# Small matrix products scheduled in unbroken blocks by tile shape, mixer sums of mixed shapes reordered, and 16- and 32-row products padded to 128 rows, in a four-layer forward pass

## The chip, the cores and the metric

The kernel runs on one core of a Trainium2 chip. A core has five engines that run at the same time and wait for each other by semaphores: TensorE (PE, matrix products, with a weight loader PEld beside it), VectorE (DVE), ScalarE (ACT), GpSimd (POOL) and SyncE (SP, which issues most DMAs). The metric is device microseconds of one execution, lower is better. Before the change the median of 3 runs is 991.59 us (989.36 to 992.03).

## The reference, cut to what matters

The input is one sequence of 256 tokens with 1024 features, all in float32. Four layers follow each other:

- Layer 1 (`even_mixer`): two recurrent mixers side by side, gated linear attention (4 heads) and RWKV-7 (8 heads with a 64x64 state each), then a SwiGLU feed-forward.
- Layer 2 (`odd_mixer`): latent attention with 16 heads, causal by chunks of 64, then a feed-forward.
- Layers 3 and 4 (`even_layer`, `odd_layer`): gated attention layers with 6 + 6 heads, or 12 heads, of 64 features, and 4 heads that attend to a memory of 256 rows.

What matters here are the small products. The RWKV-7 recurrence per head and token is

```
sa = jnp.einsum('bhvk,bhk->bhv', state, at)
state = state * wt[:, :, None, :] + sa[..., None] * bt[:, :, None, :] + vt[..., None] * kt[:, :, None, :]
y = jnp.einsum('bhvk,bhk->bhv', state, rt)
```

and attention in layers 3 and 4 is, per head, with positions turned into a bias,

```
s = softmax(q @ k.T * SCALE + bias)      # 256 queries, up to 256 keys, 64 features
o = s @ v
```

Everything else is dense projections against weights that are read from HBM.

## The kernel before, in words

The kernel is not written in the order in which it runs. Calls such as `mm1`, `V.tensor_mul` or `SC.activation` only note an operation in a `Plan` (`note`, line 222). At the end `Plan.schedule` (line 273) places all operations engine by engine in a list schedule: it keeps a clock for each engine, gives each operation a planned cost (`cost`), and picks for each free engine the ready operation with the lowest number whose tiles fit in the free buffers. Instructions are then emitted in that order, and an engine executes them in order on the chip.

Dense projections are done in `fp32r` with the weights and the activations each split in a high and a low part: `mm3` issues three products of 128x128 by up to 512 columns. Small products are single calls (`mm1`) in float32 or `fp32r`, and many of them use only a part of the 128x128 array: 64 or 32 rows of the contraction, 64 or 32 output columns. Which part is used is the tile's shape. `part_of` (line 513) gives it to the planner as rows and columns in steps of 32, 64 and 128. When the shape of an operation differs from the last one, the planner adds `TURN` nanoseconds to its cost, and while the last shape is not the full one it prefers operations of the same shape (`same_part`). Nothing forces products that were written together to run together: wide products of another stream can be placed between them.

Two streams of 128 tokens each, `stream(0)` and `stream(1)`, run interleaved, so that wide products of one fill the waits of the other. PSUM has 8 banks; `ORDER` and `CAP` say how many each group of operations may hold.

The places that the change touches:

- Low-rank gates of layer 1 (from line 1021): `w2a2` holds two 64-row weights in its halves; `g2u` holds a 32-row weight in its rows 0 to 31 and a 16-row one in rows 32 to 47. Their products use 64, 32 and 16 rows of the array.
- RWKV-7, in four chunks `c` of 64 tokens (group `R0` to `R3`): `rw_gram` (line 1202) makes the gram products of a chunk, head half 0 first and then head half 1; `rw_level` and `rw_last` invert a triangular matrix with 32x32 products; `rw_step` (line 1273) carries the state, with sums in PSUM of a 128-row product (`q["m"]` with `v_`) and a 64-row product (`blk(...)` with the old state `z`).
- Gated linear attention, `gla` (line 1362): `blocks` makes 32x32 diagonal blocks from 64-row products, five times, and further levels use similar products.
- `attend` (line 1671): for a round of heads, `points` makes the scores through `scores`, `weights` does the softmax, `turn` transposes, `values` multiplies by the values. `biased` (line 2126) and `attend_c` in `odd` give the `scores` of layers 3 and 4. Head `h` reads the row half `h % 2` of the queries and keys. For the second token tile a score has three passes (high and low parts, `dots`, line 1630).

In `points` the banks of two row halves are filled pair by pair, and inside `scores` the DVE bias follows right behind each pair:

```
for js in zip(*jobs):
    scores(js)
```

All operations on one PSUM tile follow each other in the order in which they are noted, so the second pair's products wait for the first pair's bias.

Of the kernel before, what the change touches and what calls it, by code (L numbers as in the profile page):

```python
# [19 lines left out]
P = 128  # L20
# [32 lines left out]
CAP = {("ps", "mmm"): 8, ("ps", "R0"): 1, ("ps", "R1"): 3, ("ps", "R2"): 3, ("ps", "R3"): 2, ("ps", "Bmm"): 3, ("ps", "B"): 3, ("ps", "Cmm"): 2, ("ps", "Mmm"): 2, ("ps", "M"): 1}  # L53
# [7 lines left out]
TURN = 92.0  # L61
# [119 lines left out]
class Op:  # L181
    __slots__ = ("i", "eng", "meth", "args", "kw", "cost", "dma", "succ", "need", "ready", "new", "vts", "prio",
                 "start", "end", "lab", "follow", "heavy", "busy", "table", "part", "alts", "lock")
# [22 lines left out]
class Plan:  # L206
    def __init__(self):
        self.ops, self.tiles = [], []
        self.group = "m"
        self.prio = 0.0  # L210
        self.cap = {}
        self.order = {}
# [9 lines left out]
    def note(self, eng, meth, args, kw):  # L222
# [8 lines left out]
        op.part = part_of(meth, args) if eng == "tensor" else None  # L231
        op.lock = locks(eng, meth, args, kw)
# [39 lines left out]

    def schedule(self):

        ENG = ("tensor", "vector", "scalar", "gpsimd", "sync")
# [104 lines left out]
        out, pipe, now = [], 0.0, 0.0  # L380
        warm, window, act, level, last = False, 0, {}, 0.0, 0.0
# [4 lines left out]
        while len(out) < n:  # L386
# [3 lines left out]
            for e in ENG:  # L390
                while free_at[e] <= now and (avail[e] or e in STEAL):
                    pick = None
                    if e == "tensor":
# [15 lines left out]
                    op, moved = pick, True  # L409
                    for vt in op.new:  # L410
# [440 lines left out]
def kernel(ctx: ExitStack, tc: tile.TileContext, x, xturn, pos, cols, lowr, wall, mem, memturn, ln_g, ln_b,  # L851
# [172 lines left out]
    glr = T([48, S])  # L1024
    SC.activation(glr[32:48], pss[2][32:48, 0:S], AF.Copy)
# [3 lines left out]
    sg1, sg2 = T([P, S]), T([32, S])  # L1029
# [11 lines left out]
    for j in range(2):  # L1041
        ps = g.ax()
        for d_ in range(2):
            mm1(ps[:, d_ * S:(d_ + 1) * S], w2a2[0:64, (2 * j + d_) * P:(2 * j + d_ + 1) * P], tw)
# [18 lines left out]
        ps = g.ax()  # L1063
        for d_ in range(2):
            mm1(ps[:, d_ * S:(d_ + 1) * S], w2a2[64:128, (2 * j + d_) * P:(2 * j + d_ + 1) * P], al)
# [93 lines left out]
    for j in range(2):  # L1159
# [42 lines left out]
    def rw_gram(c):  # L1202
        m_ = []
        for h in range(2):
            pa = g.ax()
            p4 = pa.rearrange("p (a b c) -> p a b c", a=4, b=2)
            for hp in range(4):
                mm1(p4[:, hp], kb(hp, c, h), blk(ar, slice(0, 2), hp, c, HS[h]))
            m_.append(T([P, 4, 2, 64]))
            V.tensor_mul(m_[h], p4, m64.unsqueeze(1).broadcast_to([P, 4, 2, 64]))  # L1210
# [24 lines left out]
    def rw_level(q, s):  # L1235
        tt = q["tt"]
        w_ = g.ax()[:, 0:P].rearrange("p (a b) -> p a b", b=32)
        for hp, h, j in quarters():
# [5 lines left out]
        for hp, h, j in quarters():  # L1244
            r_ = QS[h][j]
            mm1(d_[r_, hp], wm[r_, hp], tt[r_, 1, hp])
# [5 lines left out]
    def rw_last(q):  # L1252
# [7 lines left out]
        for hp in range(4):  # L1260
# [5 lines left out]
        for hp in range(4):  # L1266
# [6 lines left out]
    def rw_step(q, c, z, yn):  # L1273
# [3 lines left out]
        for hp in range(4):  # L1277
# [9 lines left out]
        for hp, h in PAIRS:  # L1287
# [4 lines left out]
        if c < 3:  # L1292
            pz = g.ax()
            z_ = sl4(pz)
            for hp, h in PAIRS:
# [10 lines left out]
        for hp in range(4):  # L1306
# [55 lines left out]
    def gla():  # L1362
# [11 lines left out]
        for d_ in range(2):  # L1374
            mm1(ps[:, d_ * S:(d_ + 1) * S], gw2[:, d_ * P:(d_ + 1) * P], glr[32:48])
# [18 lines left out]
        def blocks(qq, kk_, fn):  # L1394
            pss = [quarter(g.ax()), quarter(g.ax())]
            for up in range(2):
                for t in range(2):
                    for hp in range(2):
                        for d_ in range(4):
# [7 lines left out]
        for s in range(7):  # L1407
# [11 lines left out]
            if s == 5:  # L1419
# [3 lines left out]
                for t in range(2):  # L1423
# [887 lines left out]
```

## Time and profile before

| what | us |
|---|---|
| median of 3 runs | 991.59 |
| the profiled execution's own time | 986.12 |
| its span, first to last instruction | 984.3 |
| PE busy | 965.1 |
| PEld (weight loads) busy | 817.8 |
| DVE busy | 699.8 |
| ACT busy | 515.3 |
| POOL busy | 129.7 |

Busy time is the union of an engine's instructions. Matmuls overlap in the array and their ends are modelled, so a PE that is shown as busy may still be waiting inside a change of shape. How much work a stretch holds is therefore read from how many products of which shape it contains. A float32 product that is not a transpose stands in the trace as two records, an `fp32r` product or a transpose as one. [...] The mixers of layer 1 run to about 190 us, layer 2's attention lies between about 400 and 515 us, and layers 3 and 4 run from about 712 us to the end.

### The profile page before, as it was taken

To read this page: it belongs to the slowest core of one execution; us is meant where nothing else is said; L and a number is where in the kernel's file an instruction comes from. 1 tells how busy PE (TensorE), PEld (TensorE's weight loads), DVE (VectorE), ACT (ScalarE), POOL (GpSimd) and SP (SyncE) were. 2 spreads that over 40 slices of the span, in tenths; PEclk is the share of its full clock that TensorE was granted. 3 is DMA by queue.
4 is the path that set the end of the run, shared out by engine and by line. 5 is a ranking of instruction groups with operands and counts; after the bars stand their busy time and mean duration, and the time that the engine had idled before them with its cause. 6 is when DMAs were issued, how large, how long until landed. Compare 5 with 4: busy or idle time off the path is not lost.

```text
span 984.3 us, 18847 instructions
## 1 busy us (share of the span) xinstructions
PE 965.1 (98%) x7640; PEld 817.8 (83%) x7640; DVE 699.8 (71%) x1340; ACT 515.3 (52%) x995; POOL 129.7 (13%) x213
## 2 busy tenths in 40 slices
PE   8999999999999999999999999999999999999998
PEld 8977776778999988898877899988777777877777
DVE  8997988797665553876768765554689676777762
ACT  4647543545544443476653555444376664856550
POOL 1113354110000000222310000000022000122000
PEclk9999999999999999999999999999999999999999
DMA  7523434337456453544334664565542324443201
GB/s 250 215 91 136 160 134 162 135 134 256 173 196 225 177 215 112 178 140 154 129 129 169 226 247 172 174 246 181 211 160 97 129 89 170 171 171 130 83 4 44
DMA packets 27495, 156.94 MB, mean 159 GB/s; under 512 B 3424, under 2 KB 4064, under 8 KB 11664
## 3 DMA queue, kind: packets, MB, share of 16 engines
q1 hardware_dynamic: 25408, 150.49, 42.7%
q0 software_dynamic: 1280, 4.20, 1.4%
q8 instruction: 60, 0.98, 0.4%
q10 hardware_dynamic: 720, 1.05, 0.3%
q14 instruction: 27, 0.22, 0.1%
HBM read 154.68 MB, written 1.05 MB: 158 GB/s over the span
## 4 chain that ended last, share of the span: by engine, by line
PE 81%; DVE 9%; ACT 4%; DMA 4%; issue 2%; POOL 0%; SPq 0%; DVEq 0%; ACTq 0%
PE v L828 81%; DVE v L828 9%; DMA v<-in_wall 4%; ACT v L828 3%; ACT L828 1%; POOL v L828 0%; SPq L828 0%; DVEq L828 0%; ACTq L828 0%
## 5 line engine op out<-in xcount | busy, mean ns | idle before, releaser
L828 PE MATMUL v<-v,v 128*128 128x256 f32 (+14 forms) x7620 | 961.1, 295 | 14.9 <-DVE v L828 10.9
L828 PEld LDWEIGHTS v<-v,v 128*128 128x128 f32 (+7 forms) x7620 | 813.7, 164 | 162.1 <-issue 33.0
L828 DVE TENSOR_TENSOR v<-v,v 128x1024 fp32r<-128x1024 f32 (+12 forms) x609 | 462.7, 787 | 179.5 <-ACT v L828 148.1
L828 ACT ACTIVATE v<-v 128x1024 fp32r<-128x1024 f32 (+12 forms) x579 | 396.6, 717 | 355.7 <-PE v L828 180.7
L828 ACT ACTIVATE v<-v,v 128x256 f32<-128x256 f32 (+7 forms) x281 | 119.1, 455 | 96.3 <-PE v L828 67.1
L828 POOL TENSOR_TENSOR v<-v,v 128x4 f32<-128x4 f32 (+8 forms) x95 | 89.2, 951 | 557.5 <-DVE v L828 534.4
L828 DVE SCALAR_TENSOR_TENSOR v<-v,v 128x256 f32<-128x256 f32 (+7 forms) x166 | 67.6, 416 | 46.4 <-ACT v L828 27.9
L828 DVE SCALAR_TENSOR_TENSOR v<-v,v,v 128x128 fp32r<-128x128 f32 (+9 forms) x173 | 78.5, 483 | 9.7 <-PE v L828 5.4
L828 DVE TENSOR_REDUCE v<-v 128x2 f32<-128x512 f32 (+7 forms) x68 | 37.6, 566 | 15.2 <-PE v L828 9.4
L828 DVE COPY v<-v 128x512 f32<-128x512 f32 (+9 forms) x61 | 25.9, 436 | 16.6 <-PE v L828 16.0
L828 POOL DMA_DIRECT2D v<-in_ln_g x8 | 4.8, 598 | 193.1 <-PE v L828 193.1
L828 POOL TENSOR_SCALAR v<-v,v 128x128 f32<-128x128 f32 (+1 forms) x32 | 16.4, 529 | 54.1 <-DVE v L828 54.1
L828 ACT ACTIVATION_READ_ACCUMULATOR v<-v,v 128x1 f32 x96 | 20.1, 209 | 0.0
L828 DVE BATCH_NORM_STATS2 v<-v 128x6 f32<-128x64 f32 (+1 forms) x32 | 14.2, 447 | 2.8 <-PE v L828 2.7
L828 DVE TENSOR_SCALAR v<-v 128x4 f32<-128x4 f32 (+14 forms) x79 | 12.6, 177 | 2.7 <-ACT v L828 2.2
L828 DVE TENSOR_SCALAR v<-v,v 128x4 f32<-128x4 f32 (+6 forms) x42 | 10.4, 257 | 5.0 <-POOL v L828 4.4
L828 ACT ACT_TABLE_LOAD x9 | 11.5, 1283 | 0.9 <-PEq L2300 0.7
L828 POOL COPY v<-v 128x4 f32<-128x4 f32 (+2 forms) x32 | 9.8, 342 | 0.4
L828 DVE CAST v<-v 128x1024 fp32r<-128x1024 f32 (+2 forms) x14 | 8.5, 607 | 0.0
L828 DVE TENSOR_TENSOR v<-v 128x512 f32<-128x512 f32 (+4 forms) x18 | 7.6, 425 | 0.9 <-ACT v L828 0.9
L828 DVE STREAM_TRANSPOSE v<-v 128x128 f32<-128x128 f32 x20 | 5.7, 295 | 0.2
L828 PE MATMUL v<-v 128*128 128x128 f32 x20 | 4.3, 406 | 1.0 <-DVE v L828 1.0
(17 smaller groups left out, 36.1 us busy)
## 6 DMA issues: line engine op xcount, KB each, us to landing
v<-in_wall SPq DMA_DIRECT2D x123, 1024.0 KB, 4.8
v<-in_wall SPq DMA_DIRECT2D x8, 768.0 KB, 4.7
v<-in_wall SPq DMA_DIRECT2D x8, 512.0 KB, 4.3
v<-in_memturn SPq DMA_DIRECT2D x8, 256.0 KB, 5.8
v<-in_ln_g POOLq DMA_DIRECT2D x8, 256.0 KB, 4.1
v<-in_ln_b POOLq DMA_DIRECT2D x8, 256.0 KB, 5.8
v<-in_wall SPq DMA_DIRECT2D x4, 384.0 KB, 2.9
v<-in_mem SPq DMA_DIRECT2D x4, 256.0 KB, 5.5
```

Source lines behind the costliest of these rows:

```text
L828: r = getattr(getattr(nc, op.eng), op.meth)(*[real(x) for x in op.args], **{k: real(x) for k, x in op.kw.items()})
```

## The change

A context `plan.together()` marks matrix products that are noted in it as a block. Before scheduling, `join` makes the first product of a block wait for everything that any product of the block waits for, and gives it all the new tiles of the block. When the planner has placed the first product on PE, the others follow at once (`rest`), with nothing between. The price of a change of shape in the planner goes from 92 to 190, and group `R0` may hold two banks instead of one.

Blocks are put around: the low-rank products of the decay and the gate (now alternating between the two row halves), the gram products (alternating too), each half of an inversion level, each of the four groups of products in `rw_step`, the block products of `gla` (the row half is now the innermost loop), all score products of a round, and the value products of a round. The DVE bias is taken out of `scores` and noted behind the block. The output sum in `rw_step` no longer alternates between 128-row and 64-row products but does all of the one and then all of the other. The 32-row and the 16-row product become 128-row products against a tile `zlr` that is zero in the other rows, and the whole of `g2u` is loaded.

```
-CAP = {..., ("ps", "R0"): 1, ...}
+CAP = {..., ("ps", "R0"): 2, ...}
-TURN = 92.0
+TURN = 190.0
...
+        op.block = None
+        if eng == "tensor" and self.block is not None:
+            op.block = self.block
+            self.block.append(op)
...
+    @contextmanager
+    def together(self):
+        self.block = []
+        yield
+        self.block = None
+
+    def join(self):
+
+        before = {}
+        for o in self.ops:
+            for late, xs in ((True, o.succ), (False, o.follow)):
+                for x in xs:
+                    if x.block is not None and o.block is not x.block and x is not x.block[0]:
+                        before[x.block[0].i, o.i] = before.get((x.block[0].i, o.i), False) or late
+        for (i, j), late in before.items():
+            lead, o = self.ops[i], self.ops[j]
+            if lead not in (o.succ if late else o.succ + o.follow):
+                (o.succ if late else o.follow).append(lead)
+                lead.need += 1
+        for o in self.ops:
+            if o.block is not None and o is not o.block[0]:
+                o.block[0].new += o.new
+                o.new = []
+                if o not in o.block[0].succ:
+                    o.wait_for(o.block[0])
...
-                    if e == "tensor":
+                    if e == "tensor" and rest:
+                        pick = rest.pop(0)
...
+                    if op.block is not None and op is op.block[0]:
+                        rest = op.block[1:]
...
-        SP.dma_start(t_[0:(P, P, 48)[i]], lowr[i, 0:(P, P, 48)[i]])
-    gw2 = g2u[32:48, 0:256]
+        SP.dma_start(t_, lowr[i])
+    zlr = T([P, 2, S])
+    GP.memset(zlr.rearrange("p a b -> p (a b)"), 0.0)
...
-            mm1(o, g2u[0:32, (2 * j + d_) * P:(2 * j + d_ + 1) * P], sg2, False, True)
+            mm1(o, g2u[:, (2 * j + d_) * P:(2 * j + d_ + 1) * P], zlr[:, 0], False, True)
...
-        for h in range(2):
-            pa = g.ax()
-            p4 = pa.rearrange("p (a b c) -> p a b c", a=4, b=2)
-            for hp in range(4):
-                mm1(p4[:, hp], kb(hp, c, h), blk(ar, slice(0, 2), hp, c, HS[h]))
...
+        pa = [g.ax().rearrange("p (a b c) -> p a b c", a=4, b=2) for _ in range(2)]
+        with plan.together():
+            for hp in range(4):
+                for h in range(2):
+                    mm1(pa[h][:, hp], kb(hp, c, h), blk(ar, slice(0, 2), hp, c, HS[h]))
...
-        for hp in range(4):
-            for h in range(2):
-                mm1(y_[HS[h], hp], q["m"][h][:, hp, 1], v_[:, h, hp], True, c == 0)
+
+        with plan.together():
+            for hp, h in PAIRS:
+                mm1(y_[HS[h], hp], q["m"][h][:, hp, 1], v_[:, h, hp], hp == 0, c == 0 and hp == 3)
             if c:
-                for h in range(2):
-                    mm1(y_[HS[h], hp], blk(ar, 1, hp, c, HS[h]), z[HS[h], hp], False, True)
+                for hp, h in PAIRS:
+                    mm1(y_[HS[h], hp], blk(ar, 1, hp, c, HS[h]), z[HS[h], hp], False, hp == 3)
...
-            mm1(ps[:, d_ * S:(d_ + 1) * S], gw2[:, d_ * P:(d_ + 1) * P], glr[32:48])
+            mm1(ps[:, d_ * S:(d_ + 1) * S], g2u[:, d_ * P:(d_ + 1) * P], zlr[:, 1])
...
-            for js in zip(*jobs):
-                scores(js)
+            with plan.together():
+                after = [scores(js) for js in zip(*jobs)]
+            for fn in after:
+                if fn:
+                    fn()
...
-            for h0 in range(first, last, 2):
+            with plan.together():
+              for h0 in range(first, last, 2):
...
-            for h, o in jobs:
-                V.scalar_tensor_tensor(o, dist[:, P - t * P:256], slopes[h], o, op0=OP.mult, op1=OP.add)
+
+            def bias():
+                for h, o in jobs:
+                    V.scalar_tensor_tensor(o, dist[:, P - t * P:256], slopes[h], o, op0=OP.mult, op1=OP.add)
+            return bias
```

What the planner makes of it is seen in PE's order. A row is one product or several equal ones: the tile it writes, the tiles it reads, and the size of its output. The first place is the first round of scores of the second token tile in layer 3. Before, `v_8845` and `v_8847` are the banks of the two row halves, and rows of 128x512 are wide products of projections:

```order
L828 MATMUL v_8845<-v_8683,v_8769 128x256
L828 MATMUL v_8847<-v_8683,v_8769 128x256
L828 MATMUL v_8845<-v_8674,v_8790 128x256
L828 MATMUL v_8847<-v_8674,v_8790 128x256
L828 MATMUL v_8814<-v_8626,v_8421 128x512
L828 MATMUL v_8814<-v_8642,v_8421 128x512
L828 MATMUL v_8814<-v_8626,v_8430 128x512
L828 MATMUL v_8814<-v_8626,v_8421 128x512
L828 MATMUL v_8845<-v_8674,v_8769 128x256
L828 MATMUL v_8845<-v_8683,v_8769 128x256
L828 MATMUL v_8845<-v_8674,v_8790 128x256
L828 MATMUL v_8814<-v_8642,v_8421 128x512
```

Now, with `v_8856` and `v_8857` as the two banks:

```order
L868 MATMUL v_8857<-v_8674,v_8770 128x256
L868 MATMUL v_8856<-v_8683,v_8770 128x256
L868 MATMUL v_8857<-v_8683,v_8770 128x256
L868 MATMUL v_8856<-v_8674,v_8791 128x256
L868 MATMUL v_8857<-v_8674,v_8791 128x256
L868 MATMUL v_8856<-v_8674,v_8770 128x256
L868 MATMUL v_8857<-v_8674,v_8770 128x256
L868 MATMUL v_8856<-v_8683,v_8770 128x256
L868 MATMUL v_8857<-v_8683,v_8770 128x256
L868 MATMUL v_8856<-v_8674,v_8791 128x256
L868 MATMUL v_8857<-v_8674,v_8791 128x256
L868 MATMUL v_8814<-v_8626,v_8430 128x512
```

The twelve score products stood in four pieces with nine wide products between them, and two of the pieces read one row half three times in a row. They now stand in one piece and alternate.

The second place is the output sum of chunk 2 in `rw_step`. Before, `v_2693` is the sum; rows that read `v_1132`, the values, are 128-row products, one for each of two masked gram tiles, and the `x2` rows, which read the old state `v_2587`, are 64-row products:

```order
L828 MATMUL v_2693<-v_1132,v_1260 64x64
L828 MATMUL v_2693<-v_2587,v_831 64x64 x2
L828 MATMUL v_2693<-v_1132,v_1221 64x64
L828 MATMUL v_2693<-v_1132,v_1260 64x64
L828 MATMUL v_2693<-v_2587,v_831 64x64 x2
L828 MATMUL v_2693<-v_1132,v_1221 64x64
L828 MATMUL v_2693<-v_1132,v_1260 64x64
L828 MATMUL v_2693<-v_2587,v_831 64x64 x2
L828 MATMUL v_2748<-v_2443,v_2591 128x512
```

Now, with `v_2966` as the sum:

```order
L868 MATMUL v_2966<-v_1122,v_1991 64x64
L868 MATMUL v_2966<-v_1122,v_2060 64x64
L868 MATMUL v_2966<-v_1122,v_1991 64x64
L868 MATMUL v_2966<-v_1122,v_2060 64x64
L868 MATMUL v_2966<-v_1122,v_1991 64x64
L868 MATMUL v_2966<-v_1122,v_2060 64x64
L868 MATMUL v_2966<-v_1122,v_1991 64x64
L868 MATMUL v_2966<-v_1122,v_2060 64x64
L868 MATMUL v_2966<-v_2371,v_832 64x64 x8
```

The sum alternated between the two shapes in twos; it now has eight products of the one and then eight of the other.

The third place is the gram products of a chunk (`v_1949` and `v_1957` before, `v_1956` and `v_1957` now, one for each row half). Before:

```order
L828 MATMUL v_1676<-v_1653,v_217 128x512
L828 MATMUL v_1941<-v_90,v_841 128x64 x4
L828 MATMUL v_1949<-v_831,v_841 128x128 x4
L828 MATMUL v_1957<-v_831,v_841 128x128 x4
L828 MATMUL v_1966<-v_1885,v_1933 32x32 x16
```

Now:

```order
L868 MATMUL v_1956<-v_832,v_845 128x128
L868 MATMUL v_1957<-v_832,v_845 128x128
L868 MATMUL v_1956<-v_832,v_845 128x128
L868 MATMUL v_1957<-v_832,v_845 128x128
L868 MATMUL v_1956<-v_832,v_845 128x128
L868 MATMUL v_1957<-v_832,v_845 128x128
L868 MATMUL v_1956<-v_832,v_845 128x128
L868 MATMUL v_1957<-v_832,v_845 128x128
L868 MATMUL v_1976<-v_90,v_845 128x64 x4
```

Four products of one row half followed by four of the other have become eight that alternate.

## Rows read from the trace of the kernel before

**Rows 1.** The page: busy us, share of the span, instructions of each engine.

```profile
PE 965.1 (98%) x7640; PEld 817.8 (83%) x7640; DVE 699.8 (71%) x1340; ACT 515.3 (52%) x995; POOL 129.7 (13%) x213
```

**Rows 2.** Stretches: length, busy of PE, PEld, DVE, ACT, POOL, clock, DMA.

```profile
50.00:200.00 150.00, 143.91 (x2504) 112.87 (x2503) 129.44 (x322) 79.15 (x158) 48.87 (x68) 1.00 0.38 135
700.00:950.00 250.00, 247.65 (x1391) 190.90 (x1390) 190.57 (x396) 156.11 (x355) 34.83 (x35) 1.00 0.37 131
```

**Rows 3.** The chain of waits, 700 us to the end: start, us, what.

```profile
712.82 135.19 PE v L828 x735
...
872.60 108.48 PE v L828 x653
```

**Rows 4.** The chain of waits, 102 to 192 us, by line.

```profile
by line: PE v L828 91.1%; DVE v L828 5.6%; ACT v L828 2.8%; issue 1.7%
```

**Rows 5.** Whom PE waits for: us in total, times, longest.

```profile
PE v L828 <- DVE v L828: 12.0, 16, 1.3
PE v L828 <- ACT v L828: 1.8, 2, 1.4
```

**Rows 6.** Groups by shape, 690 to 700 and 600 to 620 us: busy, mean ns.

```profile
L828 PE MATMUL v<-v,v 128*128 128x512 f32 x45 | 10.6, 395 | 0.0
...
L828 PE MATMUL v<-v,v 128*128 128x256 f32 x171 | 20.4, 281 | 0.0
```

**Rows 7.** Weight loader in order of time, 745.5 to 753 us: start, us, idle before.

```profile
747.55 1.08 PEld L828 LDWEIGHTS v<-v,v 64*128 64x128 f32 x6 [0.37 <-issue]
748.99 1.20 PEld L828 LDWEIGHTS v<-v,v 64*128 64x128 f32 x8 [0.36 <-issue]
750.56 0.74 PEld L828 LDWEIGHTS v<-v,v 64*128 64x128 f32 x4 [0.37 <-DVE v L828]
751.54 1.64 PEld L828 LDWEIGHTS v<-v,v 64*128 64x128 f32 x10 [0.24 <-issue]
```

**Rows 8.** Weight loader in order of time, 166 to 173 us.

```profile
166.84 1.14 PEld L828 LDWEIGHTS v<-v,v 32*32 32x32 f32 x36 [0.36 <-DVE v L828]
168.40 1.40 PEld L828 LDWEIGHTS v<-v,v 32*32 32x32 f32 x38 [0.42 <-issue]
170.15 1.14 PEld L828 LDWEIGHTS v<-v,v 32*32 32x32 f32 x36 [0.36 <-DVE v L828]
171.66 0.34 PEld L828 LDWEIGHTS v<-v,v 32*32 32x32 f32 x32 [0.37 <-DVE v L828]
```

**Rows 9.** Groups by shape, 55.6 to 58.7 us.

```profile
L828 PE MATMUL v<-v,v 128*128 128x256 f32 x7 | 1.9, 394 | 0.0
L828 PE MATMUL v<-v,v 32*128 32x256 f32 x4 | 1.4, 426 | 0.0
```

**Rows 10.** Groups by shape, 774.59 to 775.2 (halves alternate), 750.57 to 751.05 us.

```profile
L828 PE MATMUL v<-v,v 64*128 64x256 f32 x8 | 0.7, 305 | 0.0
...
L828 PE MATMUL v<-v,v 64*128 64x256 f32 x3 | 0.6, 314 | 0.0
```

**Rows 11.** Groups by shape, 120.9 to 121.9 (one half), 136.93 to 137.5 us.

```profile
L828 PE MATMUL v<-v,v 64*128 64x128 f32 x14 | 1.5, 286 | 0.0
...
L828 PE MATMUL v<-v,v 64*128 64x128 f32 x8 | 0.7, 297 | 0.0
```

**Rows 12.** DMA issues to 60 us (KB, us to landing); GpSimd groups to 20 us.

```profile
v<-in_lowr SPq DMA_DIRECT2D x2, 256.0 KB, 5.6
v<-in_lowr SPq DMA_DIRECT2D x1, 96.0 KB, 5.1
...
L828 POOL MEMSET v<- 128x512 f32 x2 | 1.0, 522 | 0.0
```

More of the change, by code (lines that the diff above doesn't have):

```diff
@@ L182 @@
     __slots__ = ("i", "eng", "meth", "args", "kw", "cost", "dma", "succ", "need", "ready", "new", "vts", "prio",
-                 "start", "end", "lab", "follow", "heavy", "busy", "table", "part", "alts", "lock")
+                 "start", "end", "lab", "follow", "heavy", "busy", "table", "part", "alts", "lock", "block")
     def wait_for(self, other):
@@ L390, in schedule @@
             for e in ENG:
-                while free_at[e] <= now and (avail[e] or e in STEAL):
+                while free_at[e] <= now and (avail[e] or e in STEAL or e == "tensor" and rest):
                     pick = None
-                    if e == "tensor":
+                    if e == "tensor" and rest:
+                        pick = rest.pop(0)
+                        assert pick.need == 0
+                        avail[e] = [c for c in avail[e] if c[2] is not pick]
+                        heapq.heapify(avail[e])
+                    elif e == "tensor":
                         while (window + 1) * WINDOW <= now:
@@ L1061 @@
         bs.append(b_)
-        ps = g.ax()
-        for d_ in range(2):
-            mm1(ps[:, d_ * S:(d_ + 1) * S], w2a2[64:128, (2 * j + d_) * P:(2 * j + d_ + 1) * P], al)
+        ps = ps_a
         a_ = T([P, 512])
@@ L1259, in rw_last @@
         d_ = g.ax()[:, 0:P].rearrange("p (a b) -> p a b", b=32)
-        for hp in range(4):
+        with plan.together():
+          for hp in range(4):
             for h in range(2):
@@ L1265, in rw_last @@
             V.tensor_copy(wm[QS[h][1]], w_[QS[h][1]])
-        for hp in range(4):
+        with plan.together():
+          for hp in range(4):
             for h in range(2):
@@ L1276, in rw_step @@
         r0 = sl4(p0)
-        for hp in range(4):
+        with plan.together():
+          for hp in range(4):
             for h in range(2):
@@ L1286, in rw_step @@
         u_ = sl4(p1)
-        for hp, h in PAIRS:
+        with plan.together():
+          for hp, h in PAIRS:
             mm1(u_[XS[h], hp], q["tt"][XS[h], hp], r0s[XS[h], hp])
@@ L1294, in rw_step @@
             z_ = sl4(pz)
-            for hp, h in PAIRS:
+            with plan.together():
+              for hp, h in PAIRS:
                 mm1(z_[HS[h], hp], q["btk"][:, h, hp], v_[:, h, hp])
@@ L1395, in blocks @@
             pss = [quarter(g.ax()), quarter(g.ax())]
[L1396 to L1399, printed above, removed]
+            with plan.together():
+              for t in range(2):
+                for hp in range(2):
+                    for d_ in range(4):
+                        for up in range(2):
                             us, c_ = HS[up], hp * S + t * P + 32 * d_
@@ L1422, in gla @@
                 pss = [quarter(g.ax()), quarter(g.ax())]
-                for t in range(2):
+                with plan.together():
+                  for t in range(2):
                     for hp in range(2):
@@ L1434, in gla @@
             pss = [g.ax(), g.ax()]
-            for t in range(2):
+            with plan.together():
+              for t in range(2):
                 for hp in range(2):
@@ L1455, in gla @@
         pss = [g.ax(), g.ax()]
-        for hp in range(2):
+        with plan.together():
+          for hp in range(2):
             for up in range(2):
@@ L1737, in values @@
         def values(first, last):
-            for h0 in range(first, last, 2):
+            with plan.together():
+              for h0 in range(first, last, 2):
                 for j, v in enumerate(vals):
```

39 lines of the change are left out of this document (23 added, 16 removed).

## The prediction

> **What bounds the kernel now.** I read the page's busy times first, then the chain of waits, then what TensorE (PE) waits for, then groups by shape in short stretches. PE is busy for 965.1 of 984.3 us; the next engine, VectorE (DVE), for 699.8 [rows 1]. The granted clock is 1.00 in both long stretches that I use [rows 2]. In the last two layers the chain of waits is two pieces of pure PE work, 135.19 and 108.48 us [rows 3]; in the mixer stretch of layer 1, from 102 to 192 us, it is 91.1% PE [rows 4]. All of PE's visible waits for DVE and ScalarE are 13.8 us [rows 5]. So PE bounds the kernel, and what is left to explain is what fills its busy time.
>
> Steady work is cheap to price. 45 products of 512 columns take 10.6 us, 0.235 each; 171 of 256 columns take 20.4 us, 0.119 each [rows 6]. Now the attention scores of layer 3, where PE leaves its full 128x128 shape for 64-row products and comes back, four times in 4 us. The weight loads of the 64-row shape start at 747.55, 748.99, 750.56 and 751.54 us, with 0.24 to 0.37 us of idle loader ahead of each [rows 7]. By the order of PE, 2, 4 and 3 small products and 4, 4 and 1 wide ones stand in the three intervals. Two small products on different row halves run side by side and count as one of 0.12; three on one half count three times. Then:
> - 1.44 us less 0.12 and 4 x 0.235 leaves 0.38;
> - 1.57 less 0.24 and 0.94 leaves 0.39;
> - 0.98 less 0.36 and 0.235 leaves 0.385.
>
> Each interval holds one change of shape out and one back, so a change costs 0.19 to 0.20 us in which no product's steady price is paid. The profile shows it as busy, since matmuls overlap. In the mixer the same sum for 16 products of 32x32 (0.34 us by the last of the rows) and 4 wide ones gives 1.56 - 0.34 - 0.94 = 0.28 from 166.84 to 168.40 and 0.23 from 170.15 to 171.66, that is 0.12 to 0.14 a change [rows 8].
>
> **The change, part by part.** I counted changes of shape (rows and columns of the stationary operand, in steps of 32, 64 and 128) over the order of PE in both programs: 294 before, 181 after. Those to and from the 48-column products stay (10 and 8) and I leave them out. The rest: 135 to 93 in the mixers of layer 1, 22 to 24 in layer 2's attention, 127 to 56 in layers 3 and 4.
>
> *Layers 3 and 4, 71 changes fewer.* Scores of both row halves and all passes now stand in one piece, and the DVE bias comes behind the whole piece instead of between its parts. I take 0.18, just under the score price, because other excursions there are value products, whose price the rows don't show alone: 71 x 0.18 = 12.8 us. Bounds: 0.12 (8.5) and 0.20 (14.2).
>
> *Mixers, 42 fewer.* 42 x 0.14 = 5.9 us; bounds 0.115 and 0.19, 4.8 to 8.0. This holds the reordered output sums (the 128-row and 64-row products of one tile in two groups instead of alternating in twos) and the padding. The padded products, six of them, lose nothing I can see: two 32-row ones take 1.4 us among 128-row ones of which three and a half take 1.9 [rows 9], so a 32-row product of that width is no cheaper than a 128-row one; only the changes count. Bounds for the padding alone: plus 0.1 or minus 0.3 us a product.
>
> *Row halves now alternate.* Eight 64x256 products that alternate take 0.7 us, three on one half 0.6 [rows 10]: eight cost only one unit more than three. 38 score products of this kind follow one on the same half today; alternating each saves half of 0.119: 2.2 us, and about 0.5 for the float32 scores of the first token tile. In the gram products of the recurrence, seven on one half take 1.5 us and four alternating 0.7 (two records each); less 0.2 of the last one's tail in each that is 0.19 and 0.125 [rows 11]. 32 x 0.06 = 1.9 us. Bounds: nothing, and 6 us for all.
>
> *Layer 2.* Two changes more, 0.4 us.
>
> *Side edits.* The third low-rank load grows from 96 to 256 KB; the full ones land 0.5 us later [rows 12]. Its first use is the product at 56 us, so the 45 us ahead hide it; behind it on SyncE's queue stand the pieces of the next projection, and 0.5 us is its price if they were late. The new memset is like the two of 128x512 that take 1.0 us together [rows 12], on GpSimd, idle then. The larger bank limit of one group and the larger planned price of a change (TURN) only move instructions.
>
> PE's own saving is 12.8 + 5.9 + 2.2 + 0.5 + 1.9 - 0.4 = 22.9 us; with the bounds 13 to 28.
>
> *What reaches the end.* A piece's first product now waits for the latest operand of the whole piece; behind it on PE everything waits, and DVE and ScalarE wait for the scores. The planner starts a piece only when its own times say all operands are there, so most of this is covered by wide products put ahead; without that cover each wait is like today's, 12.0 us in 16, or 0.75 each [rows 5]. In layers 3 and 4 the chain is PE, DVE is busy for 190.57 of 250 us and PE for 247.65 [rows 2]: I keep 0.9 of 15.5, 14.0 us. In the mixers DVE is busy for 129.44 of 150 us [rows 2]; 7.8 us less would put it at 91%, and in the recurrence the old state's products now hold back the others of their piece. What is late next there is DVE. I keep half, 3.9. Less layer 2's 0.4: 17.5 us.
>
> Against the profiled execution, 986.12 us with a span of 984.3, that is 968.6. The median of the timed runs is 991.59, 5.5 above; on it 974.1.
>
> **The clock.** The granted clock is 1.00 in the mixer stretch though 2504 matmul records fall into 150 us [rows 2]. The longest row of products without a full-width one shrinks from 106 to 88, so nothing here asks for a lower clock. [...]
>
> **The rivals.**
> 1. *The gain turns into waits.* PE reaches each piece earlier, and its operands come from DVE and ScalarE. For it: DVE's 86% in the mixers, and that the time spent in changes covers those engines' work today. Against it: the chain is PE in layers 3 and 4. With half of 15.5 kept there and nothing in the mixers, 7.4 us: 984.2.
> 2. *All of it and a little more.* The planner now charges 190 ns a change instead of 92, near what the rows show, so its plan fits the chip better and waits shrink by up to 3 of 13.8 us: 991.6 - 25.9 = 965.7.
> 3. *Slower.* Pieces stall: 99 runs of small shapes are left (169 before), and each must hold 0.26 us of new wait to eat 22.9 and lose 3 more; or 35 waits of 0.75. The place is the recurrence, where state, DVE mask and inverse follow each other with nothing between, and the value products, which need the last transposed copy. Decides from 0.23 us a run; then 994.6.
> [...]
>
> **How the numbers follow.** Forecast 974.1 us, with 13 to 22 us gained, 0.61; rival 1, 0.20; rival 2, 0.10; rival 3, 0.04; rival 4, 0.05, of which the clock 0.02. Within 0.3%, some 3 us, a measurement of this kernel can't tell a change from none. Faster: 0.61 + 0.20 + 0.10 = 0.91; same 0.05; slower 0.04. The range runs from 964, all of 22.9 with the upper bound of a change's price, to 986, where rival 1 is nearly all in; about 0.04 lies below and 0.13 above.
>
> **What would show it.** Right: in layers 3 and 4 about 16 us less PE time for the same products, and wide products between the small ones at the steady 0.235; the mixer's end at most 8 us earlier; PE's waits for DVE up by a few us, not by 15. The four starts 1.0 to 1.6 us apart of the score loads become one. Wrong: PE's idle time up by more than 10 us, a granted clock under 1.00 in any stretch, or an interval between pieces that still holds 0.2 us a product with no change of shape in it.

## The result and the profile after

The changed kernel takes 977.15 us (median, 975.61 to 977.44), the kernel before 991.81 on the same chip; the ratio is 0.9849, 95% interval 0.9823 to 0.9875. The forecast of 974.1 was 3 us low, the range held. Stage by stage it was wrong, as the next lines show.

The page of the changed kernel, busy times (answers [rows 1]), then its instruction queue and the granted clock's stretches (answers [rows 2]; columns as there):

```profile
PE 949.1 (97%) x7640; PEld 811.6 (83%) x7640; DVE 697.1 (71%) x1340; ACT 514.8 (53%) x995; POOL 129.3 (13%) x214
...
q8 instruction: 60, 0.98, 0.4%
```

```profile
50.00:200.00 150.00, 138.40 (x2479) 110.10 (x2478) 122.62 (x311) 74.29 (x152) 45.02 (x68) 0.94 0.37 132
700.00:950.00 250.00, 247.22 (x1481) 195.75 (x1481) 196.85 (x404) 161.30 (x362) 37.60 (x35) 1.00 0.39 136
```

PE is busy for 16.0 us less, but the span falls only from 984.3 to 975.2. In the last two layers PE gets through 90 more records in the same 250 us at a clock of 1.00. In the mixer stretch it gets through 25 fewer, is busy for 5.5 us less, and the clock is 0.94 where it was 1.00.

Layer 3's scores, the weight loader from 752 us (answers [rows 7]): where four excursions stood, one stands.

```profile
751.94 4.24 PEld L868 LDWEIGHTS v<-v,v 128*128 128x128 f32 x19
756.55 3.60 PEld L868 LDWEIGHTS v<-v,v 64*128 64x128 f32 x26 [0.37 <-ACT v L868]
```

Whom PE waits for from 60 to 205 us, in the kernel before and then in the changed one (the whole span of before is in [rows 5]):

```profile
PE v L828 <- DVE v L828: 4.3, 6, 1.1
PE v L828 <- issue: 0.8, 3, 0.3
```

```profile
PE v L868 <- issue: 6.0, 3, 2.3
PE v L868 <- DVE v L868: 4.5, 8, 1.2
```

The waits for VectorE have hardly grown. New are three stalls of 6.0 us together in which PE waits for no semaphore ("issue"). The chain from 87 to 110 us has two of them:

```profile
87.42 3.93 PE v L868 x120
91.35 2.31 issue
93.66 8.91 PE v L868 x225
102.57 1.99 issue
104.56 4.71 PE v L868 x77
```

Behind each stall the granted clock drops. Stretches cut at the stalls and at the clock's own steps (clock in the third column from the end):

```profile
91.20:93.60 2.40, 0.15 (x14) 0.04 (x5) 2.02 (x3) 2.38 (x3) 0.00 (x0) 1.00 0.20 70
95.40:98.70 3.30, 3.30 (x70) 2.30 (x70) 2.22 (x5) 2.54 (x6) 1.40 (x1) 0.50 0.30 77
102.40:104.50 2.10, 0.17 (x20) 0.06 (x7) 0.74 (x1) 0.60 (x2) 1.26 (x1) 1.00 0.00 0
105.60:108.90 3.30, 3.30 (x56) 2.27 (x58) 0.76 (x2) 0.60 (x1) 0.00 (x0) 0.50 0.02 5
130.20:131.80 1.60, 0.42 (x4) 0.23 (x2) 1.60 (x3) 0.00 (x0) 1.60 (x3) 1.00 0.00 0
132.90:136.20 3.30, 3.30 (x42) 2.24 (x43) 3.30 (x7) 1.50 (x4) 0.37 (x2) 0.50 0.01 2
173.90:180.60 6.70, 6.29 (x75) 4.75 (x76) 0.69 (x2) 1.58 (x4) 0.00 (x0) 0.50 0.02 4
```

PE stands nearly idle for 1.2 to 2.3 us, and 1.7 us after the end of that at the latest it is granted half its clock (0.50), 17.1 us in all. The last row belongs to the stall at 172 us and begins 0.5 us before its end. The third of the stalls shown, at 130 us, is a wait for VectorE. The four timed executions had a mean granted clock of 0.991 to 0.993, so all of them lost about as much clock as the profiled one.

Where the stalls without a semaphore stand was the clue. PE has 15,406 records (7640 weight loads, 7640 products, 126 others) and its instruction queue brought 60 packets, one for each 257 records. The three stalls come within two records after record 1728, 2240 and 5056 in order of start, which is 192 plus a whole number of times 256; so do the three small ones of before (2752, 3520, 4800). PE went through the 256 records ahead of the three stalls in 3.57, 2.56 and 3.82 us. For the first one, the packet came only when PE already stood; the DMA queues from 83.5 to 91.2 us, then from 91.2 to 93.7 (packets, MB, share):

```profile
q1 hardware_dynamic: 198, 1.16, 42.9%
...
q1 hardware_dynamic: 90, 0.15, 17.0%
q8 instruction: 1, 0.02, 2.4%
```

The start times of these packets settle it. There is one for each border, in order, and it begins at about the time at which PE passes the border ahead. In the 14 kept executions (both kernels and the twelve runs below) PE has 37 gaps over 0.15 us without a semaphore, and every one stands at such a border. In 33 of them PE goes on 2.2 to 2.5 us after the border's packet began, in the other four 2.7 to 3.2 us after; every border that PE reached less than 1.9 us after the start of its packet has such a gap. So these gaps are waits for instructions, and such a border is called a refill border from here on. How fast PE uses up 256 records doesn't decide alone: in the changed kernel 3.55 us ahead of record 4544 passed without a gap, because the packet began 2.3 us before PE came to the border.

To locate gains I matched the full-width fp32r products of two kernels by their count and subtracted the start times; the planner moves some, so only the borders of stages are used. Microseconds ahead of the kernel before at four of its times:

| at | after | attend_only | mixer_only | tiny192 | attend34 | sums34 |
|---|---|---|---|---|---|---|
| 40 us | -1.0 | -0.2 | -1.4 | -5.5 | +0.1 | +0.6 |
| 203 us, mixers done | -7.6 | -3.6 | -7.5 | -3.8 | -1.0 | +1.0 |
| 725 us, layer 2 done | -8.5 | -6.8 | -8.8 | -5.5 | -1.8 | -1.4 |
| 960 us | +9.1 | +11.0 | -6.8 | +13.3 | +16.6 | +17.0 |

The last two layers gained 17.6 us; the mixers lost 6.6.

### The profile page after: what moved, and what is told of

Same layout as the page of the kernel before. It is cut to its first block, busy times and chain, and to the rows that moved or that the text cites. A ratio compares the mean times of both kernels' runs of the same rounds, so it can differ in the third digit from the quotient of the medians.

```text
span 975.2 us, 18832 instructions
## 1 busy us (share of the span) xinstructions
PE 949.1 (97%) x7640; PEld 811.6 (83%) x7640; DVE 697.1 (71%) x1340; ACT 514.8 (53%) x995; POOL 129.3 (13%) x214
## 4 chain that ended last, share of the span: by engine, by line
PE 73%; DVE 15%; issue 4%; ACT 3%; DMA 3%; POOL 1%; SPq 0%; DVEq 0%; POOLq 0%; ACTq 0%
PE v L868 73%; DVE v L868 15%; DMA v<-in_wall 3%; ACT v L868 3%; POOL v L868 1%; ACT L868 0%; SPq L868 0%; DVEq L868 0%; POOLq L868 0%; ACTq L868 0%
## 5 line engine op out<-in xcount | busy, mean ns | idle before, releaser
L868 PE MATMUL v<-v,v 128*128 128x256 f32 (+11 forms) x7620 | 944.8, 297 | 21.8 <-DVE v L868 13.8
L868 PEld LDWEIGHTS v<-v,v 128*128 128x128 f32 (+5 forms) x7620 | 807.3, 166 | 159.1 <-issue 34.2
L868 DVE TENSOR_TENSOR v<-v,v 128x1024 fp32r<-128x1024 f32 (+14 forms) x609 | 461.5, 784 | 185.4 <-ACT v L868 154.3
L868 ACT ACTIVATE v<-v 128x1024 fp32r<-128x1024 f32 (+15 forms) x579 | 395.8, 717 | 367.9 <-PE v L868 191.7
L868 DVE SCALAR_TENSOR_TENSOR v<-v,v 128x256 f32<-128x256 f32 (+5 forms) x166 | 67.2, 416 | 38.4 <-ACT v L868 23.1
L868 DVE TENSOR_REDUCE v<-v 128x2 f32<-128x512 f32 (+8 forms) x68 | 37.4, 565 | 14.7 <-PE v L868 9.2
L868 DVE TENSOR_SCALAR v<-v 128x4 f32<-128x4 f32 (+15 forms) x79 | 12.6, 175 | 4.5 <-ACT v L868 3.9
```

What stands on the lines that cost most here:

```text
L868: r = getattr(getattr(nc, op.eng), op.meth)(*[real(x) for x in op.args], **{k: real(x) for k, x in op.kw.items()})
```

## The experiments

The theory: the gain is made in layers 3 and 4 alone; in the mixers small products follow each other so fast that PE uses up its fetched instructions, stands for about 2 us, and then runs at half clock. The rivals: the blocks wait for operands from VectorE, or the clock falls for small products in a row as such.

**Attention alone.** The machinery for blocks and its use in `attend`; everything else as before.

```
+            with plan.together():
+                after = [scores(js) for js in zip(*jobs)]
```

> The kernel before with only the part in attention: scores and value products of layers 3 and 4 in unbroken blocks, bias behind them; mixers, planned price of a shape change and bank limits as before. Theory (the gain of the change is all in layers 3 and 4, the mixers lose by PE running out of fetched instructions and by the clock that falls after it): the order of the mixers stays the one before, no PE stall over 0.5 us without a semaphore between 60 and 210 us, granted clock 1.00, 17 to 20 us gained, all of it after 700 us: 972 to 975 us, faster than the whole change. Rival (the mixers' part is neutral, the clock's fall is only seen and costs nothing; the whole gain needs both): 977 to 981 us.

Measured: 975.28 us, ratio 0.9848 (0.9819 to 0.9878); layers 3 and 4 gained 17.8 us. That is no faster than the whole change, so the forecast for the mixers' part fell short: 3.4 us went there although their order is the one before. The weight loader of this kernel, and then of a later one with the same order there, at the same products:

```profile
135.63 0.34 PEld L868 LDWEIGHTS v<-v,v 32*32 32x32 f32 x30 [0.24 <-issue]
137.40 0.97 PEld L868 LDWEIGHTS v<-v,v 32*32 32x32 f32 x19 [1.44 <-issue]
```

```profile
136.04 0.34 PEld L868 LDWEIGHTS v<-v,v 32*32 32x32 f32 x30 [0.24 <-issue]
136.72 0.97 PEld L868 LDWEIGHTS v<-v,v 32*32 32x32 f32 x19 [0.34 <-issue]
```

The same 30 and 19 loads, an idle loader for 1.44 us in one execution and for 0.34 in the other. The place is record 4032, again 192 plus a multiple of 256; in the kernel before the packet began 0.4 us after the border ahead of it, here 2.6 us after, and 3.4 us of half clock followed. So the order before already stands near this edge.

**The mixers alone.** The same edit the other way round: the change without its part in `attend` and in the bias.

> The change without its part in attention (no blocks in scores and value products of layers 3 and 4). Theory: slower than before by 5 to 9 us (997 to 1001), granted clock 0.5 in three or four stretches between 90 and 185 us, each behind a PE stall of about 2 us. Rival (mixers neutral or a gain, hidden by something later): 984 to 991 us.

Measured: 994.51 us, ratio 1.0056 (1.0029 to 1.0082), 6 us slower than the kernel before in the same runs (988.53), as the theory had it, though the time that it named started from a slower kernel before; half clock in the same four places as in the changed kernel. By the table, layers 3 and 4 still gained 2.0 us here: with the dearer price alone there are 116 changes of shape in them instead of 127.

**The refill border moved.** Same order; the ten opening products are issued in column pieces, 46 or 56 products more.

```
+            if SPLIT and op.meth == "matmul":
+                ...
+                for u, v in zip(e, e[1:]):
+                    r = nc.tensor.matmul(o[:, u:v], a, b[:, u:v], **op.kw)
```

> The changed kernel with the same order of products, but its ten opening products (128 columns) are each issued in four or six column pieces: the same output, 46 products or 184 PE instructions more at the start. Theory (PE's instructions come in refills of 256; where a run of small products uses one up in under about 4 us PE stalls, and the granted clock then falls): with this shift no 256 instructions between two refill borders are used up in under 4.3 us by the times of the changed kernel's trace (2.6 to 3.8 in the four worst now), so the stalls at 91.2, 102.4 and 172.4 us go, the granted clock is 1.00 from 60 to 210 us, and 6 us of stalls and up to 8 us of half clock come back, less 1 to 4 us for the pieces at the start: 964 to 973 us. Rival (the clock falls because unbroken small products are too little activity, or the stalls are waits for VectorE): the same products stall, the clock falls at the same products, 977 to 981 us.

> As the run with 184 instructions more, but with six or seven pieces: 224 instructions more at the start. Theory: the stalls move to other products: the refill borders with the shortest use are now those at the products that run at 93.8, 110.4 and 168.7 us in the changed kernel's trace (3.75, 2.1 and 3.5 us), so stalls of 1 to 2.5 us stand there and none at the products of 91.2, 102.4 and 172.4; the granted clock falls behind the new ones; 974 to 981 us. Rival (activity or VectorE): stalls and clock at the same products as in the changed kernel, 977 to 981 us.

Measured: 987.19 (0.9989, 0.9974 to 1.0003) and 995.70 us (1.0076, 1.0046 to 1.0105). Both times missed, since a piece costs nearly as much as a whole opening product (24.1 us for 56 pieces, 4.6 for ten whole ones) and the start took 17 and 22 us longer. From 40 to 203 us, though, where the changed kernel falls 6.6 us behind, these gained 1.9 and lost 1.5. The same block of 32x32 products in the changed kernel and with 224 instructions more:

```profile
89.92 0.87 PEld L868 LDWEIGHTS v<-v,v 32*32 32x32 f32 x65 [0.37 <-issue]
91.03 0.21 PEld L868 LDWEIGHTS v<-v,v 32*32 32x32 f32 x14 [0.24 <-DVE v L868]
93.66 2.68 PEld L868 LDWEIGHTS v<-v,v 32*32 32x32 f32 x27 [2.42 <-issue]
```

```profile
112.08 0.87 PEld L875 LDWEIGHTS v<-v,v 32*32 32x32 f32 x65 [0.36 <-issue]
113.19 0.34 PEld L875 LDWEIGHTS v<-v,v 32*32 32x32 f32 x30 [0.24 <-DVE v L875]
116.10 2.02 PEld L875 LDWEIGHTS v<-v,v 32*32 32x32 f32 x7 [2.58 <-issue]
```

The stall moved by exactly 16 loads and 16 products, the 32 instructions by which 224 is short of 256. Its place goes by the count of instructions, not by an operand. Of the other two forecast places one stalled for 0.54 us and one not. A stall of 1.7 us stood at a border that I had not named, and it is the one of 172 us moved in the same way; in the changed kernel, then with 224 instructions more:

```profile
171.52 0.95 PEld L868 LDWEIGHTS v<-v,v 32*32 32x32 f32 x52 [0.37 <-issue]
174.31 1.87 PEld L868 LDWEIGHTS v<-v,v 64*64 64x64 f32 x29 [1.84 <-issue]
```

```profile
191.21 1.42 PEld L875 LDWEIGHTS v<-v,v 32*32 32x32 f32 x68 [0.37 <-issue]
194.48 2.60 PEld L875 LDWEIGHTS v<-v,v 64*64 64x64 f32 x52 [1.85 <-issue]
```

Again 16 loads more stand ahead of it. No half clock followed this time.

**A cheaper shift.** 48 products of 32x32 behind four of the opening ones, 192 instructions.

```
+            if op.eng == "tensor" and TINY:
+                for _ in range(TINY.pop(0)):
+                    o, a, b = (real(x)[0:32, 0:32] for x in op.args)
+                    nc.tensor.matmul(o, a, b, **op.kw)
```

> The changed kernel in its own order, with 48 products of 32x32 (192 PE instructions) put among its ten opening products, twelve behind each of four of them; the output is the same. By the steady 0.017 us such a product costs, with eight changes of shape, the start is 1 to 3 us longer (the column pieces cost 20). By the trace of the changed kernel no 256 instructions between two refill borders are then used up in under 4.38 us. Theory (refills): the stalls without a semaphore at 91, 102 and 172 us go, half clock stays at most behind one wait for VectorE, the mixers take 7 to 9 us less than in the changed kernel: 969 to 973 us, faster than the changed kernel though it does more. Rival (operands, or too little activity in unbroken small products): stalls and half clock at the same products, 978 to 981 us.

Measured: 975.31 us, ratio 0.9862 (0.9835 to 0.9890). The start cost 4.5 us, not 1 to 3, so the total missed its range and is hardly ahead; the mixers took 8.3 us less than in the changed kernel, as forecast. The mean granted clock of the six executions is 0.996 to 0.998. The block from above, whole, then whom PE waits for from 60 to 205 us, and two stretches:

```profile
94.40 0.87 PEld L868 LDWEIGHTS v<-v,v 32*32 32x32 f32 x65 [0.37 <-issue]
95.51 0.57 PEld L868 LDWEIGHTS v<-v,v 32*32 32x32 f32 x33 [0.25 <-DVE v L868]
```

```profile
PE v L868 <- DVE v L868: 6.0, 9, 1.2
PE v L868 <- issue: 1.9, 2, 1.3
```

```profile
101.00:107.00 6.00, 5.46 (x175) 4.12 (x174) 5.91 (x13) 2.47 (x5) 1.76 (x2) 1.00 0.54 178
131.50:134.80 3.30, 3.30 (x17) 2.53 (x13) 3.27 (x8) 1.86 (x4) 0.90 (x4) 0.50 0.01 2
```

The same unbroken blocks run at a clock of 1.00 once PE doesn't run dry (175 product records in the 6 us from 101 us); only the half clock behind the wait for VectorE at 130 us is left there. A stall of 1.3 us stands at 173 us, at another border than before. Both rivals fall for the three stalls. Of the 8.3 us, 4.1 are stalls (6.0 less 1.9), while PE's waits for VectorE rose by 1.5 (from 4.5 to 6.0). That the other 4 to 6 us go with the 13.7 us less at half clock (17.1 less 3.4) is worked out, not measured alone.

**No blocks, a slower pace, a lower price.** Blocks in the mixers off (`loose_mixer`); then with a rule that puts a full-width product first when many PE instructions were just placed (`paced_loose`); the rule with blocks on (`paced_blocks`); blocks with the old price of a change (`price92`).

```
-        with plan.together():
+        with nullcontext():
```

```
+                        crowded = done > SPENT and now - spent[0][0] < PACE
+                        if crowded:
+                            pick = best(e, heavy_of)
```

```
-TURN = 190.0
+TURN = 92.0
```

> The changed kernel without its blocks in the mixers of layer 1 (nothing there is bound to run unbroken; the reordered sums, the padding, the alternating row halves, the planned price of 190 ns and the blocks in attention stay). The planner, by its price alone, makes 179 changes of shape, as few as with blocks (181). Theory (what hurts is many small products in a row, by a block or not: PE runs out of fetched instructions): it doesn't help; one to four PE stalls of 1 to 2.5 us without a semaphore between 85 and 205 us, the granted clock at half behind them, 972 to 981 us. Rival (the blocks hurt because a piece waits for the last of its operands): without them the mixers gain 4 us or more, no stall over 1 us, 964 to 971 us.

> The same kernel (no blocks in the mixers) with one rule more in the planner: when 230 PE instructions were placed in the last 4 us of its clock, a full-width product goes first if there is one. By the steady prices of the trace 256 PE instructions in a row then take 3.8 us at the least (1.8 without the rule, 1.3 in the changed kernel); it makes 219 changes of shape, 38 more than the changed kernel. Theory: no PE stall over 0.7 us without a semaphore, granted clock 1.00 from 60 to 210 us but for what a wait for VectorE brings; the mixers' 7 to 8 us of loss come back, less 38 x 0.14 = 5 us that are gained no more: by the attention part's 17.7, a mixer part of 0 to +4 and 2 to 3 lost in layer 2, 967 to 974 us, 2 to 8 us faster than the unpaced one. Rival (operands or activity): stalls and clock as without the rule, and 5 us more for the changes: 978 to 986 us.

> The changed kernel, blocks and all, with the same kind of rule (200 instructions in 5 us): a block starts only when PE has not used up that many just before, if a full-width product can go first. 192 changes of shape; 14 places instead of 288 where 256 instructions in a row take under 3 us by the steady prices, 176 instead of 854 under 3.6. Theory: at most one stall over 1 us without a semaphore between 85 and 205 us, granted clock at half in at most one stretch for that cause, 966 to 974 us. Rival: as the changed kernel, 976 to 982 us.

> The changed kernel with the planner's price of a change of shape left at 92 ns (the blocks alone make 182 changes). Theory (the blocks, not the price, bring the small products together): stalls of the same kind at refill borders, clock under 1.00 between 90 and 205 us, 973 to 982 us. Rival (it is the dearer price, which also counts as activity in the planner's clock, that lets the clock fall): granted clock 1.00 and 966 to 971 us.

Measured: 977.42 (0.9869, 0.9839 to 0.9899), 977.14 (0.9860, 0.9834 to 0.9887), 984.02 (0.9934, 0.9909 to 0.9960) and 984.26 us (0.9942, 0.9916 to 0.9969). Taking the blocks off changed nothing that can be measured in the whole; in the profiled execution the mixers lose 1.7 us from 40 to 203 us instead of 6.6, but from 203 to 725 us 4.8 are lost instead of 0.9, which no run explains. The stalls at the borders are there without blocks as well, so blocks aren't needed for them, and with the old price too, so the dearer price isn't either. The old price made the kernel slower than forecast; why wasn't tried. Whom PE waits for from 60 to 205 us without blocks, then with blocks and the old price:

```profile
PE v L868 <- issue: 5.3, 4, 3.5
PE v L868 <- DVE v L868: 4.5, 5, 1.7
```

```profile
PE v L868 <- issue: 7.6, 4, 3.8
PE v L868 <- DVE v L868: 4.2, 8, 0.9
```

The pacing rule did what it was to do and still missed its times: with it no such stall exceeds 0.7 us. Without blocks, PE's waits for VectorE stayed as they were (13.0 us over the whole span), but 13.7 us of half clock stand behind waits for VectorE and ScalarE, and there are 38 changes of shape more. With blocks the waits grew. With blocks and the rule, whom PE waits for over the whole span, and a wait with what follows:

```profile
PE v L877 <- DVE v L877: 22.5, 24, 3.4
```

```profile
148.00:151.20 3.20, 1.00 (x49) 0.72 (x43) 2.89 (x6) 1.45 (x3) 3.01 (x8) 1.00 1.01 382
151.30:158.00 6.70, 6.40 (x59) 4.93 (x58) 5.50 (x23) 1.08 (x2) 2.52 (x5) 0.50 0.24 70
```

PE waits 22.5 us for VectorE instead of 14.8, and the clock falls behind such a wait as it does behind the stalls without a semaphore: PE is idle for 2.2 of the 3.2 us from 148 us, and 0.50 follows for 6.7 us. So in these runs half clock stands behind an idle PE, whatever it waits for, though not each time: in the run with the old price a stall of 2.0 us at 150 us brought no half clock. That the wide products placed early are the ones missing later is likely, but not shown.

**Blocks in layers 3 and 4 alone.** Layer 2's use of `attend` goes without; in the kernel with attention alone, and in the one with 48 small products.

```
+        whole = plan.together if rows else nullcontext
```

> The kernel before with blocks only in the attention of layers 3 and 4, not in layer 2. Theory (layer 2's blocks make PE wait for ScalarE and VectorE and lose 2 to 3 us between 525 and 600 us): 2 to 3 us faster than with all of attention, 970 to 973 us by a kernel before of 990; the gain from 725 us on is 17 to 18 us as in every run with blocks there. Rival (layer 2's blocks are free): same as with all of attention, 973 to 976 us.

> Both together: the whole change with 48 products of 32x32 at the start and no blocks in layer 2. Theory: the two gains add, 966 to 971 us, faster than both kernels. Rival: 976 to 981 us.

Measured: 969.08 us, ratio 0.9806 (0.9775 to 0.9838), and 975.73 us, 0.9867 (0.9840 to 0.9894). The first came out 1 us better than its range; its median is the lowest of the study, though the kernel of the next experiment can't be told from it. Between 525 and 700 us it loses 0.3 us where attention alone lost 2.4. The rest of its lead over that one is mostly in the mixers, where the stall at record 4032 shrank to 0.2 us in this execution. Its mean granted clock is 1.000 in four of six executions; with all of attention it is 0.994 to 0.998. In the other pair layer 2's blocks made no difference: with the whole change PE waits 1.7 us for VectorE there with or without them. The two gains don't add (it isn't known why), and what layer 2 loses under the higher price isn't due to its blocks.

**One part of the mixers' change on top.** In layer 1 only the output sums in two groups, no blocks.

```
+            for hp, h in PAIRS:
+                mm1(y_[HS[h], hp], q["m"][h][:, hp, 1], v_[:, h, hp], hp == 0, c == 0 and hp == 3)
```

> The kernel with blocks only in the attention of layers 3 and 4, and one part of the mixers' change without blocks: the output sums of the recurrence in two groups (all 128-row products of a tile, then all 64-row ones) instead of alternating in twos; planned price 92 ns, no padding, no other reordering. 208 changes of shape instead of 225, and no more places than before where 256 PE instructions in a row are small (260 under 3.0 us by steady prices in both). Theory (fewer changes pay in the mixers too, where they don't bring small products closer together): 17 x 0.14 = 2.4 us faster than with attention alone, 965 to 969 us by a kernel before of 988 to 990, granted clock 1.00. Rival (in the mixers VectorE takes back what PE saves, as half of the forecast had it): the same as with attention alone, 968 to 972 us.

Measured: 970.98 us, ratio 0.9816 (0.9791 to 0.9842), no different from the one without. By 203 us it is 2.0 us further ahead (0.5 of that by 40 us), near the 2.4 of the theory, by 250 us it has lost that again. The weight loader, and the stretch of the wait:

```profile
200.59 5.58 PEld L868 LDWEIGHTS v<-v,v 128*128 128x128 f32 x26 [0.25 <-issue]
208.82 0.42 PEld L868 LDWEIGHTS v<-v,v 128*128 128x128 f32 x4 [2.66 <-issue]
```

```profile
205.00:215.00 10.00, 7.72 (x30) 5.85 (x30) 10.00 (x17) 4.30 (x6) 1.00 (x1) 0.83 0.51 193
```

VectorE is busy all through these 10 us: PE comes earlier to products that wait for it, stands for 2.2 us, and then has 3.4 us of half clock. In this execution saved PE time turned into a wait, as the rival had it.

## Why the prediction was right and where it was wrong

- *What bounds the kernel.* Right: PE is busy for 97% after.
- *Layers 3 and 4.* The mechanism held: the four excursions became one, the clock stayed at 1.00, PE's waits for VectorE from 700 us on went from 2.3 to 2.8 us. The term was sized too low: 14.0 us kept, 17.6 measured (17.8 to 18.8 in four other kernels). Less the 2.7 for alternating halves, 14.9 over 71 changes is 0.21 us each, just above my upper bound of 0.20, and VectorE took next to nothing back; the factor 0.9 had no ground. But where only the planned price cut changes there (`mixer_only`), 11 fewer brought 2.0 us, 0.18 each, which is what I took; the excess may as well lie in the alternation. How the sum splits wasn't tried.
- *Mixers.* The step that failed: 7.8 us saved, half kept, 3.9 gained; measured 6.6 lost between 40 and 203 us. What failed was not the cost of a change nor the waits for VectorE, but the sentence that nothing asks for a lower clock since the longest row of products without a full-width one shrinks. I counted products, not the time in which PE uses up its instructions. The three small "issue" gaps of before, all at refill borders, were in the trace, and the argument left them out. No run shows that the length of such a row sets the clock. It fell to 0.50 behind an idle PE (stalls of 1.2 to 2.3 us) and not for unbroken small products: with the border moved the same ones ran at 1.00. There the mixers gain 1.7 us with the same blocks (1.9 with 184 instructions more), of the sign that was forecast and less than half of its size; a stall of 1.2 to 1.3 us and 3.4 us of half clock are left in both.
- *Layer 2.* 0.4 us forecast, 0.9 measured from 203 to 725 us.
- *The sum.* The profiled execution of before was 5.5 us under its median, that of the changed kernel (977.35) on its own. Against the former the gain is 8.8 us, not 17.5; against the medians 14.7. By the table, layers 3 and 4 gave 3.6 us more than forecast, the mixers 10.5 less, layer 2 another 0.5 less, and 1.0 went by 40 us: 9.1. That the total still came near the forecast is luck: the median of before was high. In the four later sets of runs its median is 987.7 to 989.7, by which the gain would be 11 to 13 us. Those executions, 56 in all, also show that its time goes with the clock: the 21 at a mean granted clock of 1.000 took 985.4 to 989.7 us, the 11 at 0.993 to 0.996 988.4 to 995.2. So its longer executions run in part at a lower granted clock; whether behind stalls at refill borders, as the run with attention alone does in the same order, no trace shows.
- *The range.* Its lower end was added up wrongly: with the upper bounds of a change's price the saving is 26.4 us, which gives 965, not 964.
- *Rivals.* Of rival 4's chance of 0.05, 0.02 was for a falling clock in the mixers. No row of before shows a clock under 1.00 or what it costs; in the changed kernel 17.1 us ran at 0.50, behind stalls that no rival named, and cost some 5 to 7 us (an estimate, from the 4 to 6 us that go with 13.7 us of half clock above). Of the signs named for a wrong forecast one showed, a clock under 1.00; PE's idle time rose by 6.9 us, under the 10 named.

## What to carry to other kernels

Blocks of small products gained 17.6 us here in layers 3 and 4, where PE never waited for instructions, and the mixers lost 6.6 us with three such waits of 6.0 us. So count instructions, not products (a float32 product is four records here, an fp32r one two), and look in the trace at each 256th record for gaps with no semaphore: all 37 of this study stood there. Move the border by some harmless instructions before blaming operands: with 224 more, two stalls moved along with the count, by 16 loads each, and so were waits for instructions. And a stall of 2 us on PE may cost as much again in granted clock (an estimate, from the run with 48 small products: 4.1 us were stalls, another 4 to 6 us go with the clock), so an edit that saves 2 us and opens a new wait can give nothing: `sums34` was 2.0 us further ahead by 203 us and had lost that by 250 us.

## What the runs showed of the hardware that was not expected

- PE can outrun its instruction supply. In the changed kernel 256 records in 2.56 to 3.82 us led to stalls of 1.7 to 2.3 us. Over the runs, 3.06 us passed without one and 4.04 us led to one of 2.0 us (both in `price92`, records 1472 and 4032): what counts is the start of the packet, 2.2 to 2.5 us after which PE goes on in 33 of 37 gaps. The 60 packets for 15,406 records and the borders 256 records apart agree with refills of 256 instructions. In the changed kernel 57 of 60 borders were crossed without a gap; at the other three PE stood for 6.0 us. Why a packet begins 0.6 us before PE passes a border in one place and 3.9 us after it at the next (records 1216 and 1472 of the changed kernel) stays open.
- Not every stall of PE brings half clock: a wait of 1.2 us for VectorE at 130 us did in the changed kernel, stalls of 1.7 us (224 instructions more) and 2.0 us (old price) did not.
- An opening product of 21 to 32 columns costs nearly as much as one of 128: 56 pieces took 24.1 us, 0.43 each, the ten whole ones 4.6 us, 0.46 each. Why wasn't tried.
